# Hybrid streaming encoder step: fewer pieces made early at a mixer's end, an earlier reciprocal, and sums of squares on one engine

## The chip, the cores and the metric

The kernel runs on one core of one Trainium2 chip. A core has a matmul engine (PE), three engines for elementwise work (DVE, ACT, POOL), and queues for transfers; SP's queue carries nearly all weight loads here. Each engine works through its own instructions strictly in program order and waits on semaphores for the others. The metric is device time in microseconds; the kernel before takes 1227.7 us (median of 3 runs, 1226.74 to 1227.85).

## The reference

One inference step of a two-layer trunk over 304 tokens (16 meta, 256 prompt, 32 sample), width 1024, in fp32. Cut to what matters here:

```python
def half_ffn(x, g_pre, w_in, w_out, g_post):
    gate, up = jnp.split(rmsnorm(x, g_pre) @ w_in, 2, axis=-1)
    return x + 0.5 * rmsnorm((jax.nn.silu(gate) * up) @ w_out, g_post)

for l in range(DEPTH):                                   # DEPTH = 2
    x = half_ffn(x, norm_ffn1_pre[l], ffn1_w_in[l], ffn1_w_out[l], norm_ffn1_post[l])
    z = rmsnorm(x, norm_mix_pre[l]) @ w_in[l]            # attention q k v, retention q k v, gate
    mix = concat(windowed_attention(z), groupnorm(retention(z)) * silu(gate))
    x = x + rmsnorm(mix @ w_out[l], norm_mix_post[l])
    x = half_ffn(x, norm_ffn2_pre[l], ffn2_w_in[l], ffn2_w_out[l], norm_ffn2_post[l])
y = rmsnorm(x, final_norm)                               # plus caches and retention states
```

Every sub-layer ends with an RMS norm of its output, so its sum of squares over all 1024 features must be known before the residual can be formed, and the next sub-layer starts with another norm.

## The kernel before

**Pieces.** Activations lie transposed, features on the 128 partitions and tokens along the free axis. A weight comes from memory in chunks of 128x1024 fp32 (tile `raw`, 4 buffers, so a load can only start when both halves of the chunk four places ahead of it have been read). Each half of a chunk is a piece of 128x512. A piece is made by two instructions: ACT writes a rounded copy `hi` (line 206) and DVE the rest `lo = raw - hi` (line 209). PE multiplies every piece in three passes, weights hi with activations hi (line 258), lo with hi (259), hi with lo (261). Pieces go into a ring of 10 buffers and at most 8 may lie made and unused. For the places where one sub-layer ends and the next begins, extra buffers are opened (`xhi`, `xlo`), so that the first `EXTRA` pieces of the next sub-layer can be made early on top of the ring's 8; that number is line 68, and `edges` lists the four places.

**Order of the work.** The Python program writes instructions in its own order, and each engine keeps that order. `tick` advances a model clock after each step of matmuls, lets `advance` make the next pieces, and runs what has fallen due in the list `later`. So where pieces are made decides what stands in front of the norm's instructions in ACT's and DVE's queues.

**End of a mixer** (function `mixer`). The two gate products (`done_g`) are followed by `gate_out`: for each of four blocks ACT applies silu, DVE multiplies (line 1147), ACT copies to hi (1148), DVE forms lo (1149). Then come two groups of matmuls with `w_out`, each over eight blocks of the input (the four attention blocks first, the four gated ones last) and four output blocks. `Post.done0` handles the first group's outputs as they finish: ACT squares (512), DVE scales by the norm's gain (513), POOL adds the squares into `acc` (515). `Post.done1` does so for the second group, with the additions on DVE (525, 527). `finish` sums over the partitions with four matmuls of ones (533, 534), split around PE's matmuls for the retention state (line 826: 8 ahead, 56 behind). After that `pre_norm` of the next sub-layer follows: POOL scales x by s (547), DVE and ACT form the new activations (562, 565, 425, 428).

**The factor s.** x is kept multiplied by the norm's s for a while, and `unscale` divides it out again: a reciprocal on DVE (line 571, tile `rs`), and eight products on POOL (line 574, one per block of x). In a mixer, `unscale` stands after `gate_out`; in the feed-forwards it runs out of the list `later`, or in the last one before the third group of matmuls.

Of the kernel before, what the change touches and what calls it, by code (L numbers as in the profile page):

```python
# [12 lines left out]
ALU = mybir.AluOpType  # L13
# [51 lines left out]
R_NORM = 2663  # L65
R_KT = 7100
UNSCALE = 1500
EXTRA = 8
RAWS = 4


# [36 lines left out]
def tile_hybrid_step(ctx, tc, I, O):  # L108
    nc = tc.nc
    PE, ACT, DVE, POOL, SP = nc.tensor, nc.scalar, nc.vector, nc.gpsimd, nc.sync  # L110
# [11 lines left out]
    chunks = []  # L122
# [22 lines left out]
    edges = []  # L145
    for l in range(DEPTH):
        if l:
            edges.append(2 * len(chunks))
        ch_ffn_in(I["ffn1_w_in"][l])
        ch_cols(I["ffn1_w_out"][l], 512, KF)  # L150
        ch_cols(I["ffn1_w_out"][l], 0, KF)
        edges.append(2 * len(chunks))
        ch_qkv(I["w_in"][l])
        for c0 in (C_Q + 256, C_RK, C_RQ, C_RV, C_RK + 256, C_RQ + 256, C_RV + 256, C_G, C_G + 256):
            ch_pair(I["w_in"][l], c0)
        ch_cols(I["w_out"][l], 512, KD)
        ch_cols(I["w_out"][l], 0, KD)
        edges.append(2 * len(chunks))
        ch_ffn_in(I["ffn2_w_in"][l])
        ch_cols(I["ffn2_w_out"][l], 512, KF)  # L160
        ch_cols(I["ffn2_w_out"][l], 0, KF)


    extra = {b + j for b in edges for j in range(EXTRA)}
    ring = [0]
    for i in range(2 * len(chunks)):
        ring.append(ring[-1] + (i not in extra))
# [62 lines left out]
    clock = [0.0]  # L230
    later = []
# [205 lines left out]
    def small(name, tag=None, bufs=1):  # L437
        return ap.tile([P, N], F32, tag=tag or name, bufs=bufs, name=name)
# [59 lines left out]
    T0 = 0  # L498


    class Post:
        def __init__(self, post, nxt):
            self.post, self.nxt = post, nxt
            self.yg = acts(4, F32)
            self.acc = small("acc")
            self.b2 = None
            self.last = None

        def done0(self, m, bk):
            y = bk[m][:, :N - T0]  # L510
            sq = ap.tile([P, N], F32, tag="sq", bufs=2, name="sq") if m else self.acc
            ACT.activation(out=sq[:, T0:], in_=y, func=ACTF.Square)  # L512
            DVE.tensor_scalar(out=self.yg[m][:, T0:], in0=y, scalar1=gain(*self.post, 4 + m), scalar2=None, op0=ALU.mult)
            if m:
                POOL.tensor_tensor(out=self.acc[:, T0:], in0=self.acc[:, T0:], in1=sq[:, T0:], op=ALU.add)  # L515

        def done1(self, m, bk):
            self.bk = bk
# [41 lines left out]
        def step(self, k):  # L560
# [5 lines left out]
            if k == KD - 1:  # L566
                ACT.activation(out=self.se[:, T0:], in_=self.s[:, T0:], func=ACTF.Square, scale=EPS ** 0.5)

        def unscale(self):
            rs = small("rs")  # L570
            DVE.reciprocal(out=rs[:, T0:], in_=self.s[:, T0:])  # L571

            def part(k):
                POOL.tensor_tensor(out=x[:, k, T0:], in0=x[:, k, T0:], in1=rs[:, T0:], op=ALU.mult)  # L574
            for k in range(KD):
                later.append((clock[0] + UNSCALE * k, lambda k=k: part(k)))
            later.sort(key=lambda e: e[0])


    def ffn(pre, post, nxt, prev, after=None):  # L580
# [5 lines left out]
        with tc.tile_pool(name="ffn", bufs=1, reuse_waits="tile") as fp, ExitStack() as late:  # L586
# [22 lines left out]
            for g in range(KF // 2):  # L609
                if g == 1:  # L610
# [6 lines left out]
                    for j in range(2):  # L617
                        pair(0, j, bk)
                if g == 2 and prev and last:
                    prev.unscale()  # L620
                if g == 2 and not prev:
                    late_loads()
# [3 lines left out]
                    fin.x_in(*divmod(g - 4, 2))  # L626
                bk = group4(KD, xh, xl, n, (0, 2, 1, 3), done(g), lead=2 if prev and g == 0 else 1)
            if prev and not last:
                later.append((clock[0] + UNSCALE, prev.unscale))
            if not last:  # L630
                open_extra()
            p = Post(post, nxt)
# [101 lines left out]
    def mixer(l, prev):  # L734
# [431 lines left out]
        if lastl:  # L1166
            T0 = NMETA
        n = N - T0
        group2(xh, xl, n, done_g(0))
        group2(xh, xl, n, done_g(1))  # L1170
        flush()
# [1 line left out]
        mtmp.close()  # L1173
        open_extra()
        prev.unscale()
        p = Post((3, l), (4, l))
        ox, lx = (lambda k: mh[k][:, T0:]), (lambda k: ml[k][:, T0:])
        group4(KD, ox, lx, n, range(4), p.done0)
        ACT.preload_act_table(ACTF.Sqrt)
# [12 lines left out]
    prev = None  # L1192
# [32 lines left out]
```

## Time and profile before

| | |
|---|---|
| median of 3 runs | 1227.7 us |
| profiled execution: time, span | 1228.38 us, 1226.6 us |
| PE busy | 1179.8 us, 96% of the span |
| DVE busy | 825.1 us, 67% |
| ACT busy | 593.7 us, 48% |
| POOL busy | 193.0 us, 16% |
| TensorE clock granted, mean | 0.986 of full |
| DMA | 182.51 MB, 149 GB/s over the span |

PE is busy nearly all the time, so time is lost or won where PE stands still or runs at its lower clock. The span is 1.8 us shorter than the execution's own time, and that time 0.7 us above the median.

### The profile page before, as it was taken

Reading aid. Unit: us, or ns where it says so; the run is one execution under the profiler, and the core shown is the slowest. Engines: PE = TensorE matmul, PEld = TensorE weight load, DVE = VectorE, ACT = ScalarE, POOL = GpSimd, SP = SyncE. Lnnn points to the kernel's source line nnn. Section 1 sums busy time; section 2 is a strip of 40 time slices with the busy share of each in tenths; the row PEclk is TensorE's granted clock in tenths of the full one; section 3 lists DMA queues with packets and bytes.
Section 4 is the critical chain, followed back from the end, with each engine's and each line's share of the span. In section 5 each row is a group of like instructions: output and inputs, shape, how many; then the busy total and the mean of one; then the engine's idle time right before and its main releaser. Section 6 shows DMA issues by size and latency. Waiting matters only on the chain. (4 is left out here: it accounts for less than half of the span.)

```text
span 1226.6 us, 22759 instructions
## 1 busy us (share of the span) xinstructions
PE 1179.8 (96%) x8716; PEld 1148.3 (94%) x8716; DVE 825.1 (67%) x1491; ACT 593.7 (48%) x1211; POOL 193.0 (16%) x205
## 2 busy tenths in 40 slices
PE   8999999999997999999999999999999879999995
PEld 8999999998896999999989999998989869999995
DVE  6766654677777766665576665757767877766543
ACT  6544544555446544444454444455544554554442
POOL 4200001220234300013030000313111443000000
PEclk9999999999998999999999999999999989999997
DMA  7655465723425364545716455556344435645531
GB/s 223 173 178 164 138 189 157 240 74 114 124 87 172 87 189 138 159 157 165 224 36 189 138 158 182 161 162 201 108 108 117 123 118 151 205 140 173 188 104 39
DMA packets 155309, 182.51 MB, mean 149 GB/s; under 512 B 12016, under 2 KB 125984, under 8 KB 154944
## 3 DMA queue, kind: packets, MB, share of 16 engines
q1 hardware_dynamic: 153488, 178.84, 47.8%
q0 software_dynamic: 1344, 1.76, 0.8%
q8 instruction: 68, 1.11, 0.4%
q10 hardware_dynamic: 368, 0.47, 0.1%
q14 instruction: 41, 0.34, 0.1%
HBM read 175.70 MB, written 2.23 MB: 145 GB/s over the span
## 5 line engine op out<-in xcount | busy, mean ns | idle before, releaser
L209 DVE TENSOR_TENSOR lo<-raw,hi 128x512 fp32r<-128x512 f32 x608 | 419.1, 733 | 131.8 <-ACT hi L206 128.0
L258 PE MATMUL bk<-act,hi 128*128 128x304 f32 (+1 forms) x1664 | 504.8, 305 | 0.3 <-ACT act L425 0.3
L259 PE MATMUL bk<-act,lo 128*128 128x304 f32 (+1 forms) x1664 | 496.0, 300 | 0.8 <-DVE lo L209 0.8
L261 PE MATMUL bk<-act,hi 128*128 128x304 f32 (+1 forms) x1664 | 479.1, 300 | 1.3 <-DVE act L428 1.3
L206 ACT ACTIVATE hi<-raw 128x512 fp32r<-128x512 f32 x607 | 348.1, 622 | 143.4 <-PE bk L261 104.7
L258 PEld LDWEIGHTS bk<-act,hi 128*128 128x128 f32 x1664 | 312.9, 188 | 5.9 <-issue 3.5
L259 PEld LDWEIGHTS bk<-act,lo 128*128 128x128 f32 x1664 | 313.0, 188 | 2.0 <-DVE lo L209 1.5
L261 PEld LDWEIGHTS bk<-act,hi 128*128 128x128 f32 x1664 | 306.7, 188 | 2.0 <-DVE act L428 2.0
L258 PE MATMUL bk<-hh,hi 128*128 128x304 f32 (+1 forms) x704 | 210.7, 300 | 0.0
L259 PE MATMUL bk<-hh,lo 128*128 128x304 f32 (+1 forms) x704 | 210.2, 299 | 0.0
L261 PE MATMUL bk<-hl,hi 128*128 128x304 f32 (+1 forms) x704 | 207.8, 301 | 0.0
L595 ACT ACTIVATE sg<-tg 128x304 f32<-128x304 f32 (+1 forms) x88 | 40.0, 455 | 199.6 <-DVE tg L594 199.6
L258 PEld LDWEIGHTS bk<-hh,hi 128*128 128x128 f32 x704 | 132.5, 188 | 0.0
L259 PEld LDWEIGHTS bk<-hh,lo 128*128 128x128 f32 x704 | 132.3, 188 | 0.0
L261 PEld LDWEIGHTS bk<-hl,hi 128*128 128x128 f32 x704 | 131.0, 188 | 0.0
L594 DVE TENSOR_TENSOR tg<-bk,rb 128x304 f32<-128x304 f32 (+1 forms) x88 | 41.0, 466 | 86.3 <-PE bk L261 86.1
L574 POOL TENSOR_TENSOR x<-x,rs 128x304 f32<-128x304 f32 (+1 forms) x40 | 46.6, 1197 | 309.6 <-DVE rs L571 309.6
L599 DVE TENSOR_TENSOR hl<-tu,hh 128x304 fp32r<-128x304 f32 (+1 forms) x88 | 41.5, 471 | 50.9 <-ACT hh L598 45.0
L598 ACT ACTIVATE hh<-tu 128x304 fp32r<-128x304 f32 (+1 forms) x88 | 40.0, 455 | 59.5 <-DVE tu L597 59.5
L515 POOL TENSOR_TENSOR acc<-acc,sq 128x304 f32<-128x304 f32 (+1 forms) x18 | 15.7, 870 | 322.6 <-ACT sq L512 321.8
L547 POOL TENSOR_TENSOR x<-x,s 128x304 f32<-128x304 f32 (+1 forms) x35 | 31.3, 930 | 140.9 <-PE bk L295 109.3
L258 PE MATMUL bk<-act,xhi 128*128 128x304 f32 (+1 forms) x160 | 49.6, 315 | 2.8 <-ACT act L425 2.6
(239 smaller groups left out, 1116.5 us busy)
## 6 DMA issues: line engine op xcount, KB each, us to landing
raw<-in_ffn_w_in_dram SPq DMA_DIRECT2D x352, 256.0 KB, 4.7
raw<-in_ffn_w_out_dram SPq DMA_DIRECT2D x88, 512.0 KB, 4.9
raw<-in_w_in_dram SPq DMA_DIRECT2D x36, 512.0 KB, 4.1
raw<-in_w_out_dram SPq DMA_DIRECT2D x16, 512.0 KB, 3.8
raw<-in_w_in_dram SPq DMA_DIRECT2D x16, 256.0 KB, 3.1
dec<-in_dec_dram SPq DMA_DIRECT2D x2, 1280.0 KB, 8.3
t<-t SPq DMA_DIRECT2D x24, 76.0 KB, 2.1
out_dram<-xgm SPq DMA_DIRECT2D x2, 384.0 KB, 3.6
```

The source lines that it names most:

```text
L206: ACT.activation(out=hi, in_=r, func=ACTF.Copy)
L209: DVE.tensor_tensor(out=lo, in0=r, in1=hi.bitcast(F32), op=ALU.subtract)
L258: PE.matmul(out=out, lhsT=a, rhs=xh, start=first, stop=False)
L259: PE.matmul(out=out, lhsT=b, rhs=xh, start=False, stop=False)
L261: PE.matmul(out=out, lhsT=a, rhs=xl, start=False, stop=last)
L515: POOL.tensor_tensor(out=self.acc[:, T0:], in0=self.acc[:, T0:], in1=sq[:, T0:], op=ALU.add)
L547: POOL.tensor_tensor(out=x[:, j, T0:], in0=x[:, j, T0:], in1=self.s[:, T0:], op=ALU.mult)
L574: POOL.tensor_tensor(out=x[:, k, T0:], in0=x[:, k, T0:], in1=rs[:, T0:], op=ALU.mult)
L594: DVE.tensor_tensor(out=tg[:, T0:], in0=bk[j][:, :n], in1=rb[:, T0:], op=ALU.mult)
L595: ACT.activation(out=sg[:, T0:], in_=tg[:, T0:], func=ACTF.Silu)
L598: ACT.activation(out=hh[a][:, T0:], in_=tu[:, T0:], func=ACTF.Copy)
L599: DVE.tensor_tensor(out=hl[a][:, T0:], in0=tu[:, T0:], in1=hh[a][:, T0:].bitcast(F32), op=ALU.subtract)
```

## The change

Three edits. The edge at a mixer's end gets 4 extra pieces, the other edges keep 8. `unscale` is cut in two: `inverse` makes the reciprocal, and in a mixer it is now written in front of the gate's matmuls, with the eight products where they were; in the feed-forwards that use `later`, the reciprocal stays at its time and the products come one step of 1500 model ns behind it. And `Post` takes the engine for the additions in `done0`; a mixer passes DVE.

```diff
--- before.py
+++ after.py
@@ -65,7 +65,7 @@
 R_NORM = 2663
 R_KT = 7100
 UNSCALE = 1500
-EXTRA = 8
+EXTRA = (8, 4)
 RAWS = 4
 
 
@@ -145,23 +145,23 @@
     edges = []
     for l in range(DEPTH):
         if l:
-            edges.append(2 * len(chunks))
+            edges.append((2 * len(chunks), EXTRA[0]))
         ch_ffn_in(I["ffn1_w_in"][l])
         ch_cols(I["ffn1_w_out"][l], 512, KF)
         ch_cols(I["ffn1_w_out"][l], 0, KF)
-        edges.append(2 * len(chunks))
+        edges.append((2 * len(chunks), EXTRA[0]))
         ch_qkv(I["w_in"][l])
         for c0 in (C_Q + 256, C_RK, C_RQ, C_RV, C_RK + 256, C_RQ + 256, C_RV + 256, C_G, C_G + 256):
             ch_pair(I["w_in"][l], c0)
         ch_cols(I["w_out"][l], 512, KD)
         ch_cols(I["w_out"][l], 0, KD)
-        edges.append(2 * len(chunks))
+        edges.append((2 * len(chunks), EXTRA[1]))
         ch_ffn_in(I["ffn2_w_in"][l])
         ch_cols(I["ffn2_w_out"][l], 512, KF)
         ch_cols(I["ffn2_w_out"][l], 0, KF)
 
 
-    extra = {b + j for b in edges for j in range(EXTRA)}
+    extra = {b + j for b, e in edges for j in range(e)}
     ring = [0]
     for i in range(2 * len(chunks)):
         ring.append(ring[-1] + (i not in extra))
@@ -499,8 +499,8 @@
 
 
     class Post:
-        def __init__(self, post, nxt):
-            self.post, self.nxt = post, nxt
+        def __init__(self, post, nxt, eng=POOL):
+            self.post, self.nxt, self.eng = post, nxt, eng
             self.yg = acts(4, F32)
             self.acc = small("acc")
             self.b2 = None
@@ -512,7 +512,7 @@
             ACT.activation(out=sq[:, T0:], in_=y, func=ACTF.Square)
             DVE.tensor_scalar(out=self.yg[m][:, T0:], in0=y, scalar1=gain(*self.post, 4 + m), scalar2=None, op0=ALU.mult)
             if m:
-                POOL.tensor_tensor(out=self.acc[:, T0:], in0=self.acc[:, T0:], in1=sq[:, T0:], op=ALU.add)
+                self.eng.tensor_tensor(out=self.acc[:, T0:], in0=self.acc[:, T0:], in1=sq[:, T0:], op=ALU.add)
 
         def done1(self, m, bk):
             self.bk = bk
@@ -566,12 +566,13 @@
             if k == KD - 1:
                 ACT.activation(out=self.se[:, T0:], in_=self.s[:, T0:], func=ACTF.Square, scale=EPS ** 0.5)
 
+        def inverse(self):
+            self.rs = small("rs")
+            DVE.reciprocal(out=self.rs[:, T0:], in_=self.s[:, T0:])
+
         def unscale(self):
-            rs = small("rs")
-            DVE.reciprocal(out=rs[:, T0:], in_=self.s[:, T0:])
-
             def part(k):
-                POOL.tensor_tensor(out=x[:, k, T0:], in0=x[:, k, T0:], in1=rs[:, T0:], op=ALU.mult)
+                POOL.tensor_tensor(out=x[:, k, T0:], in0=x[:, k, T0:], in1=self.rs[:, T0:], op=ALU.mult)
             for k in range(KD):
                 later.append((clock[0] + UNSCALE * k, lambda k=k: part(k)))
             later.sort(key=lambda e: e[0])
@@ -617,6 +618,7 @@
                     for j in range(2):
                         pair(0, j, bk)
                 if g == 2 and prev and last:
+                    prev.inverse()
                     prev.unscale()
                 if g == 2 and not prev:
                     late_loads()
@@ -626,7 +628,8 @@
                     fin.x_in(*divmod(g - 4, 2))
                 bk = group4(KD, xh, xl, n, (0, 2, 1, 3), done(g), lead=2 if prev and g == 0 else 1)
             if prev and not last:
-                later.append((clock[0] + UNSCALE, prev.unscale))
+                later.append((clock[0] + UNSCALE, prev.inverse))
+                later.append((clock[0] + 2 * UNSCALE, prev.unscale))
             if not last:
                 open_extra()
             p = Post(post, nxt)
@@ -1166,6 +1169,7 @@
         if lastl:
             T0 = NMETA
         n = N - T0
+        prev.inverse()
         group2(xh, xl, n, done_g(0))
         group2(xh, xl, n, done_g(1))
         flush()
@@ -1173,7 +1177,7 @@
         mtmp.close()
         open_extra()
         prev.unscale()
-        p = Post((3, l), (4, l))
+        p = Post((3, l), (4, l), DVE)
         ox, lx = (lambda k: mh[k][:, T0:]), (lambda k: ml[k][:, T0:])
         group4(KD, ox, lx, n, range(4), p.done0)
         ACT.preload_act_table(ACTF.Sqrt)
```

The first place is DVE at the end of the first mixer, from the gate's last instruction to the last pieces of `w_out`; `osb` is the retention output, `act` an activation buffer. Before:

```order
L1149 TENSOR_TENSOR act<-osb,act 128x304
L571 RECIPROCAL rs<-s 128x304
L209 TENSOR_TENSOR lo<-raw,hi 128x512 x6
L513 TENSOR_SCALAR act<-bk,gcol 128x304 x4
L209 TENSOR_TENSOR lo<-raw,hi 128x512 x2
```

And now, with line numbers moved by the new lines:

```order
L1152 TENSOR_TENSOR act<-osb,act 128x304
L209 TENSOR_TENSOR lo<-raw,hi 128x512 x6
L513 TENSOR_SCALAR act<-bk,gcol 128x304 x2
L515 TENSOR_TENSOR acc<-acc,sq 128x304
L513 TENSOR_SCALAR act<-bk,gcol 128x304
L515 TENSOR_TENSOR acc<-acc,sq 128x304
L513 TENSOR_SCALAR act<-bk,gcol 128x304
L515 TENSOR_TENSOR acc<-acc,sq 128x304
L209 TENSOR_TENSOR lo<-raw,hi 128x512 x2
```

The reciprocal has left this place (it stands in front of the last retention blocks now), and three additions have come from POOL.

The second place is ACT in the second group of `w_out`, from the extra pieces to the norm's square root (line 538). Before:

```order
L206 ACTIVATE xhi_4599<-raw 128x512
L206 ACTIVATE xhi_4603<-raw 128x512
L206 ACTIVATE hi<-raw 128x512 x4
L525 ACTIVATE sq<-bk 128x304
L206 ACTIVATE hi<-raw 128x512 x2
L525 ACTIVATE sq<-bk 128x304 x3
L206 ACTIVATE hi<-raw 128x512 x2
L538 ACTIVATE bk<-bk,epst 128x304
```

And now:

```order
L206 ACTIVATE xhi_4553<-raw 128x512
L206 ACTIVATE xhi_4557<-raw 128x512
L206 ACTIVATE hi<-raw 128x512 x6
L525 ACTIVATE sq<-bk 128x304 x4
L206 ACTIVATE hi<-raw 128x512 x2
L538 ACTIVATE bk<-bk,epst 128x304
```

In front of the last of the four squares stood 8 extra and 6 ring pieces; now it is 4 and 6. The four pieces that are left over come after the statistics of the next sub-layer, in front of its first gate products.

The third place is POOL, from its last product of the group norm (`gsd` is that norm's factor) to the next sub-layer. Before:

```order
L925 TENSOR_TENSOR osb<-osb,gsd 128x304 x3
L574 TENSOR_TENSOR x<-x,rs 128x304 x7
L515 TENSOR_TENSOR acc<-acc,sq 128x304
L574 TENSOR_TENSOR x<-x,rs 128x304
L515 TENSOR_TENSOR acc<-acc,sq 128x304 x2
L521 TENSOR_SCALAR xg<-x,gcol 128x304
```

And now:

```order
L800 TENSOR_TENSOR qr<-t_3961,t_3963 128x608
L928 TENSOR_TENSOR osb<-osb,gsd 128x304 x3
L575 TENSOR_TENSOR x<-x,rs 128x304 x8
L521 TENSOR_SCALAR xg<-x,gcol 128x304
L547 TENSOR_TENSOR x<-x,s 128x304 x7
```

The eight products of x follow straight on the group norm, with no additions among them.

## Rows read from the trace of the kernel before

**Rows 1.** Who waited for whom: total us, times, longest us.

```profile
PE bk L533 <- DVE acc L527: 19.0, 5, 9.5
```

**Rows 2.** Timeline of PE, first mixer's end: start, us, instruction, [idle before, releaser].

```profile
358.94 0.30 PE L261 MATMUL bk<-act,hi 128*128 128x304 f32 x1
...
372.55 0.41 PE L259 MATMUL bk<-act,lo 128*128 128x304 f32 x1 [0.24 <-DVE lo L209]
...
375.30 0.30 PE L261 MATMUL bk<-act,hi 128*128 128x304 f32 x1
375.54 0.68 PE L826 MATMUL bk<-vt,k 128*64 128x64 f32 x8
384.86 1.38 PE L533 MATMUL bk<-acc,ones 128*128 128x304 f32 x2 [8.64 <-DVE acc L527]
...
406.10 0.30 PE L258 MATMUL bk<-act,hi 128*128 128x304 f32 x1
```

**Rows 3.** Timeline of PE, second mixer's end.

```profile
975.08 0.40 PE L259 MATMUL bk<-act,lo 128*128 128x288 f32 x1 [0.53 <-DVE lo L209]
...
988.12 1.33 PE L533 MATMUL bk<-acc,ones 128*128 128x288 f32 x2 [9.53 <-DVE acc L527]
```

**Rows 4.** Timeline of PE, end of the first feed-forward.

```profile
234.79 0.30 PE L261 MATMUL bk<-hl,hi 128*128 128x304 f32 x1
235.38 0.78 PE L533 MATMUL bk<-acc,ones 128*128 128x304 f32 x2 [0.28 <-DVE acc L527]
...
255.50 0.30 PE L258 MATMUL bk<-act,hi 128*128 128x304 f32 x1
```

**Rows 5.** Timeline of ACT, first mixer's end.

```profile
369.11 0.42 ACT L512 ACTIVATE sq<-bk 128x304 f32<-128x304 f32 x1 [7.54 <-POOL acc L515]
...
371.89 3.24 ACT L206 ACTIVATE xhi<-raw 128x512 fp32r<-128x512 f32 x6
...
378.47 0.63 ACT L206 ACTIVATE hi<-raw 128x512 fp32r<-128x512 f32 x1 [1.51 <-DMA raw<-in_ffn_w_in_dram]
...
381.43 0.41 ACT L525 ACTIVATE sq<-bk 128x304 f32<-128x304 f32 x1
```

**Rows 6.** Timeline of DVE, from the last retention blocks to the next feed-forward.

```profile
334.43 0.69 DVE L209 TENSOR_TENSOR lo<-raw,hi 128x512 fp32r<-128x512 f32 x1 [2.29 <-ACT hi L206]
...
352.34 0.46 DVE L1147 TENSOR_TENSOR osb<-osb,zg 128x304 f32<-128x304 f32 x1
...
357.54 0.47 DVE L1149 TENSOR_TENSOR act<-osb,act 128x304 fp32r<-128x304 f32 x1 [0.53 <-ACT act L1148]
357.93 2.04 DVE L571 RECIPROCAL rs<-s 128x304 f32<-128x304 f32 x1
359.90 6.87 DVE L209 TENSOR_TENSOR lo<-raw,hi 128x512 fp32r<-128x512 f32 x6
366.69 1.41 DVE L513 TENSOR_SCALAR act<-bk,gcol 128x304 f32<-128x304 f32 x3
...
413.10 0.48 DVE L599 TENSOR_TENSOR hl<-tu,hh 128x304 fp32r<-128x304 f32 x1 [3.08 <-POOL qr L843]
...
416.00 3.70 DVE L209 TENSOR_TENSOR lo<-raw,hi 128x512 fp32r<-128x512 f32 x6
```

**Rows 7.** Timeline of POOL, first mixer's end.

```profile
349.70 0.84 POOL L925 TENSOR_TENSOR osb<-osb,gsd 128x304 f32<-128x304 f32 x1 [4.00 <-DVE gsd L924]
360.06 8.22 POOL L574 TENSOR_TENSOR x<-x,rs 128x304 f32<-128x304 f32 x7 [9.52 <-DVE rs L571]
```

**Rows 8.** Timeline of DVE, a sum and a product with both inputs in SBUF.

```profile
394.43 1.11 DVE L565 TENSOR_TENSOR x<-x,act 128x304 f32<-128x304 f32 x1
...
1037.17 0.81 DVE L597 TENSOR_TENSOR tu<-tu,sg 128x288 f32<-128x288 f32 x1 [0.21 <-ACT sg L595]
```

**Rows 9.** Stretches: us, busy (count) of PE, PEld, DVE, ACT, POOL, PEclk, DMA share, GB/s.

```profile
376.00:385.00 9.00, 0.36 (x5) 0.22 (x3) 6.91 (x12) 6.19 (x13) 0.00 (x0) 0.73 0.98 304
385.00:391.00 6.00, 6.00 (x61) 4.78 (x62) 3.51 (x7) 2.24 (x5) 2.10 (x3) 0.55 0.78 240
```

## The prediction

> **What bounds the kernel now.** PE is busy 96% of the span, so I looked for the places where it is not. The list of waits comes first: of all waits on PE the longest by far is that of the norm's sum (L533) for the additions of squares on DVE (L527), 19.0 us over five times, none above 9.5 [rows 1]. The timeline of PE says which ones matter: 8.64 us at the first mixer's end, 9.53 at the second's [rows 2, 3], against 0.28 at a feed-forward's end [rows 4], where the same instructions stand. So two places hold nearly all of PE's idle time, and the reader is to see that in each PE has finished its matmuls (last of them at 375.30) and has only eight small ones left to do until 384.86.
>
> What is late there is read on ACT. The square of block 0 comes at 381.43, though its bank was complete some 2.5 us ahead of 375.30. In front of it in ACT's queue are a square that waited 7.54 us for POOL's additions, until 369.11, then two pieces, eight extra pieces and four more, the latter also waiting for their loads [rows 5]; two more stand between the squares. DVE shows why all began late: the gate ends at 357.54, then come a reciprocal of 2.04 us and six pieces that take 6.87 us, while six pieces elsewhere take 3.70 [rows 6]. Beside the 6.87 POOL runs its products of x, seven in 8.22 us [rows 7]. DVE and POOL hinder each other there.
>
> The wait has a second price. In the 9 us of it the granted clock is 0.73, in the 6 us behind it 0.55, near the lower of the two levels (1.2 against 2.4 GHz) [rows 9]. From L533 to the ninth piece of the next sub-layer takes 406.10 - 384.86 = 21.24 us here, 255.50 - 235.38 = 20.12 where PE had hardly stood still [rows 2, 4].
>
> **The change part by part.** All times are of the first mixer; both ends have the same shape.
>
> *What PE would need if nothing were late.* Last matmul at 375.30, less its own stall of 0.24 on a piece [rows 2], is 375.06. To L533 a feed-forward takes 235.38 - 234.79 = 0.59 [rows 4], and the eight state matmuls 0.68 [rows 2]: 376.33. That is 8.5 us before 384.86, the most that this end can give by itself.
>
> *Reciprocal moved.* It leaves the place behind the gate, where 2.04 us stood on the path. It now stands in front of the retention blocks, some 6 us before the idle 2.29 us of DVE at 334.43 [rows 6], which takes it up; PE needs the results pushed by it only several us later. Cost 0, and 2.0 each if that cover is gone.
>
> *Products of x moved.* They no longer wait for the reciprocal, so POOL starts them when its last group-norm product ends, 349.70 + 0.84 = 350.54 instead of 360.06 [rows 7]. The six pieces behind the gate are freed (6.87 to 3.70). But the products now run beside the gate. Eight of them at 0.84 (alone) to 1.17 (8.22/7) take 6.7 to 9.4 us; at 1.1, until 359.4. The gate's eight DVE instructions, 352.34 to 358.01, take two SBUF inputs each. No row has them beside a busy POOL. The nearest rows: the gate's own take 0.46 alone [rows 6], others of their kind 1.11 or 0.81 beside POOL [rows 8], so 0.35 to 0.65 more for each; 0 is the bound below (an overlap can't make them faster). I take 0.5, between the two rows, for the six that fall before 359.4: the gate ends at 361.0. PE wants its last result at 358.94 [rows 2], so the margin is 0.93 and PE stalls 3.0 - 0.9 = 2.1 us, and so do the matmuls behind it. Bounds: 0, and 8 x 0.65 - 0.9 = 4.3.
>
> The Trainium skill, page "SBUF — State Buffer", section "Who interferes with whom", has a rule that speaks against this edit: a DVE instruction with two SBUF inputs and a GpSimd instruction that reads SBUF exclude one another for a whole instruction, and whichever started first goes first. The trace agrees as far as it goes: DVE's scalings of PSUM (one SBUF input at most) run at 1.41/3 = 0.47 beside POOL [rows 6], while the pieces nearly double. By the rule a gate instruction could wait a whole product of 0.84, eight of them 6.7 us, and the stall would be 5.8 instead of at most 4.3, some 1.5 us per mixer more.
>
> *Additions on DVE.* POOL's additions are gone, and with them ACT's wait until 369.11. DVE gets three more at about 0.47. Now the last square of the first group waits for DVE: six pieces from 361.0 (3.7), two scalings and an addition (1.4), 366.1, still 3.0 earlier.
>
> *Four early pieces fewer.* From that square ACT then has 12.3 us of work and waits to 381.43 before, and 4 pieces fewer now in front of the first squares, with two more moved ahead of them; by 0.4 for the square, 1.1 for two pieces, 1.3 for the table load behind them, and ten pieces at 3.24/6 = 0.54, it can be at the squares at 374.3 plus what it waits for loads. Loads can start some 2 us earlier, as raw buffers are freed earlier, and five chunks instead of seven must arrive before the last square. Waits on loads in front of the squares were about 2 us (one of 1.51 [rows 5]); I keep 2: 376.3. PE's last matmul starts at 375.06 + 2.1 = 377.2, so ACT is just in time for the last block. DVE, with pieces and additions one behind another, adds some 0.5 at the end. L533 starts at 376.33 + 2.1 + 0.5 = 378.9, 5.9 us earlier.
>
> *Where the four pieces go.* They stand between the reciprocal of the next norm and the first gate product of the feed-forward, about 4 x 0.62 = 2.5 us on DVE. Behind them the third of the products there waited 3.08 us for POOL's state until 413.10 [rows 6]; that wait shrinks by what they take, so the pieces of 416.00 stay where they were. From 358.94 to 375.30 PE starts 114 matmuls, 16.12 us without the stall, 0.141 each [rows 2]. It needs the first of the four when its ninth to twelfth pieces are through, 4 x 12 matmuls behind 406.10, at 412.9; they are made by about 411. Cost 0; 2.5 per mixer if the wait on POOL gave nothing, and still behind PE's margin.
>
> *Clock.* PE no longer stands 8.6 us, so the stretch behind L533 should come to the 20.12 of the feed-forward: 1.1 us.
>
> *Feed-forwards.* The products come one step later in a group of 22 pieces, 264 matmuls at 0.141, 37 us, in which POOL is otherwise idle: 0.
>
> *Sum.* First mixer 5.9 + 1.1 = 7.0. The second waited 0.9 longer (9.53 against 8.64) and stalled 0.53 on a piece instead of 0.24, which goes too: 7.0 + 0.9 + 0.3 = 8.2. Together 15.2 us. The profiled execution took 1228.4 (span 1226.6), 0.7 above the median of 1227.7; from the median I forecast 1212.5.
>
> **The rivals.** *Gate undisturbed:* POOL and DVE miss one another, as the gate's instructions start 1.4 us apart with gaps. Then the 2.1 and the 0.5 fall away: 8.5 + 1.1 = 9.6 and 10.8, 20.4 us, 1207.3. Against it: POOL's products have no gaps, and every two-input instruction beside such a row was slower [rows 8]. *Gate at its worst:* 4.3 instead of 2.1 on each, 10.8 us in all, 1217; by the page's rule 1.5 more each, 1220.
>
> *Loads decide:* at 376 to 385 the DMA engines are 98% busy at 304 GB/s [rows 9]. If the squares still wait for their chunks, only the four pieces (2 chunks of 0.52 MB, 3.4 us at 304 GB/s) are saved, with 1.1 for the clock, so 4.5 each, 9 us, 1218.7. Against it: until the pieces behind the gate are read no load can start for want of buffers, and that moves forward.
>
> *The edit of the pieces does nothing but move them:* PE then waits for the first pieces of the feed-forward instead. Four pieces late by their whole time on DVE, 2.5 us, and the wait on POOL not hiding them: 15.2 - 5 = 10, 1217.5. The margin of 1.9 us at 412.9 speaks against it.
>
> *Slower:* the stall in the gate lets the clock fall. The second group of `w_out` is 96 matmuls at 0.141 us, 13.5 us, and twice that at half the clock. If it stayed low through all of it, L533 would come at 378.9 + 13.5 = 392.4, 7.5 later than before; without the 1.1, 7.5 and 6.3 us, 1241.5. It decides from about 6 us of low clock in that group. Against it: stalls of 0.24 and 0.53 left the clock alone, and 2.1 is nearer to these than to 8.64. The Trainium skill, "TensorE: Matmul & The Clock Gate", section "Loop structure matters more than you think", warns of waits between bursts of matmuls; which of the two a 2 us stall is, no row here shows.
>
> **How the numbers follow.** Forecast (1209 to 1216 around 1212.5): 0.55. Gate undisturbed: 0.17. Gate at its worst, loads, or late pieces, 1216 to 1221: 0.20. No change or little of it, by two of these at once: 0.04. Slower: 0.04. The range from 1205.5 to 1219.5 leaves out the last two and the tail of the third. 0.2% is 2.5 us, about what a measurement of this kernel tells from no change: faster 0.92, the same 0.04, slower 0.04.
>
> **What would show it.** Right: PE's idle time before L533 at 1 to 3 us at both mixer ends; granted clock near 1 behind it; the six pieces behind the gate at about 3.7 us; POOL's products starting at the last group-norm product; the gate's DVE instructions at 0.8 to 1.1 us and PE stalling about 2 us in the last blocks of the first `w_out` group. Wrong: L533 still waiting 5 us or more; a stall of PE in the first two groups of a second feed-forward; a granted clock of about one half in the second `w_out` group.

## The result, and the profile after

The changed kernel takes 1210.58 us (median of 4 runs, 1210.19 to 1211.73) against 1227.23 for the kernel before (4 runs, 1226.74 to 1227.85): a ratio of 0.9866, 95% interval 0.9849 to 0.9883. The forecast was 1212.5, the range 1205.5 to 1219.5. The profiled execution took 1210.19 us, its span is 1208.4 instead of 1226.6, the mean granted clock 0.995 instead of 0.986. Line numbers behind line 569 are up to 3 higher than before.

The list of waits on PE (total us, times, longest) shows the norm's sum, 19.0 us in [rows 1], at 2.3, and one new entry: the first matmul that uses a gated block waits for ACT's rounded copy of it.

```profile
PE bk L533 <- DVE acc L527: 2.3, 4, 1.4
PE bk L258 <- ACT act L1151: 1.7, 2, 0.9
```

The timeline of PE at the first mixer's end (start, us, instruction, idle before it and what ended it) has the new stall in the first `w_out` group, and no idle time at all ahead of L533, where 8.64 us stood [rows 2]. The row of 396.52 is the next sub-layer's ninth piece.

```profile
358.95 0.41 PE L258 MATMUL bk<-act,hi 128*128 128x304 f32 x1 [0.87 <-ACT act L1151]
...
375.42 0.30 PE L261 MATMUL bk<-act,hi 128*128 128x304 f32 x1
...
376.31 0.78 PE L533 MATMUL bk<-acc,ones 128*128 128x304 f32 x2
...
396.52 0.30 PE L258 MATMUL bk<-act,hi 128*128 128x304 f32 x1
...
952.83 0.40 PE L258 MATMUL bk<-act,hi 128*128 128x288 f32 x1 [0.80 <-ACT act L1151]
...
970.84 0.75 PE L533 MATMUL bk<-acc,ones 128*128 128x288 f32 x2 [1.40 <-DVE acc L527]
```

From 952.83 it is the second mixer: the same stall, and 1.40 us in front of L533 instead of 9.53 [rows 3].

ACT's timeline says why. The fourth square of the first group waits 1.59 us instead of 7.54 [rows 5]; from there to the second group's squares it has two pieces, a table load and ten more pieces, and loses 0.73 us to a load; and the last two squares wait for PE's matmuls. At the second mixer (967.21) the last two pieces wait 1.53 us for their load, and the third square then waits for DVE: from this come the 1.40.

```profile
364.54 0.42 ACT L512 ACTIVATE sq<-bk 128x304 f32<-128x304 f32 x1 [1.59 <-DVE acc L515]
...
372.60 1.39 ACT L206 ACTIVATE hi<-raw 128x512 fp32r<-128x512 f32 x2 [0.73 <-DMA raw<-in_ffn_w_in_dram]
373.89 0.72 ACT L525 ACTIVATE sq<-bk 128x304 f32<-128x304 f32 x2
375.19 0.42 ACT L525 ACTIVATE sq<-bk 128x304 f32<-128x304 f32 x1 [0.58 <-PE bk L259]
375.77 0.42 ACT L525 ACTIVATE sq<-bk 128x304 f32<-128x304 f32 x1 [0.16 <-PE bk L261]
...
967.21 1.37 ACT L206 ACTIVATE hi<-raw 128x512 fp32r<-128x512 f32 x2 [1.53 <-DMA raw<-in_ffn_w_in_dram]
...
969.76 0.41 ACT L525 ACTIVATE sq<-bk 128x288 f32<-128x288 f32 x1 [0.59 <-DVE acc L527]
```

DVE's timeline has the reciprocal in its new place (327.86) with idle time still left behind it (0.83 us at 333.70; 2.29 before, [rows 6]). In the gate the products (L1150) of blocks 2 to 4 take 1.11 us instead of 0.46, while the subtractions (L1152) keep about 0.5. The six pieces behind the gate take 3.70, not 6.87. In the next feed-forward the 3.08 us wait for POOL [rows 6] is gone: L600 there waits 0.58 us, for ACT.

```profile
327.86 2.05 DVE L571 RECIPROCAL rs<-s 128x304 f32<-128x304 f32 x1
...
351.60 0.59 DVE L1150 TENSOR_TENSOR osb<-osb,zg 128x304 f32<-128x304 f32 x1
...
353.15 1.11 DVE L1150 TENSOR_TENSOR osb<-osb,zg 128x304 f32<-128x304 f32 x1
354.78 0.52 DVE L1152 TENSOR_TENSOR act<-osb,act 128x304 fp32r<-128x304 f32 x1 [0.52 <-ACT act L1151]
355.23 1.11 DVE L1150 TENSOR_TENSOR osb<-osb,zg 128x304 f32<-128x304 f32 x1
...
358.93 0.47 DVE L1152 TENSOR_TENSOR act<-osb,act 128x304 fp32r<-128x304 f32 x1 [0.52 <-ACT act L1151]
359.45 3.70 DVE L209 TENSOR_TENSOR lo<-raw,hi 128x512 fp32r<-128x512 f32 x6
...
404.14 0.48 DVE L600 TENSOR_TENSOR hl<-tu,hh 128x304 fp32r<-128x304 f32 x1 [0.58 <-ACT hh L599]
...
407.05 3.70 DVE L209 TENSOR_TENSOR lo<-raw,hi 128x512 fp32r<-128x512 f32 x6
```

POOL's timeline, asked for in narrow stretches so that each product of x has a row of its own, has them straight behind the group norm. Those beside the gate take 1.07, where one of this size alone takes 0.84 [rows 7].

```profile
352.86 1.07 POOL L575 TENSOR_TENSOR x<-x,rs 128x304 f32<-128x304 f32 x1
353.89 1.08 POOL L575 TENSOR_TENSOR x<-x,rs 128x304 f32<-128x304 f32 x1
354.93 1.07 POOL L575 TENSOR_TENSOR x<-x,rs 128x304 f32<-128x304 f32 x1
```

The stretches of [rows 9] (us, busy and count of PE, PEld, DVE, ACT, POOL, granted clock, DMA share, GB/s) have PE at work and the clock at its upper level, 2.4 GHz, in all three; the first row is the second `w_out` group, behind the stall in the gate.

```profile
369.00:376.00 7.00, 7.00 (x55) 6.82 (x54) 6.35 (x12) 5.36 (x11) 0.00 (x0) 1.00 0.86 265
376.00:385.00 9.00, 8.50 (x93) 6.85 (x91) 7.18 (x13) 4.11 (x10) 5.69 (x7) 1.00 0.62 201
385.00:391.00 6.00, 5.87 (x40) 5.62 (x41) 5.96 (x9) 3.31 (x8) 4.89 (x6) 1.00 0.00 0
```

### The profile page after: what moved, and what is told of

Same layout as the page of the kernel before. It is cut to its first block, busy times and chain, and to the rows that moved or that the text cites. A ratio compares the mean times of both kernels' runs of the same rounds, so it can differ in the third digit from the quotient of the medians.

```text
span 1208.4 us, 22774 instructions
## 1 busy us (share of the span) xinstructions
PE 1177.9 (97%) x8716; PEld 1146.5 (95%) x8716; DVE 823.1 (68%) x1497; ACT 593.0 (49%) x1211; POOL 185.4 (15%) x199
## 3 DMA queue, kind: packets, MB, share of 16 engines
q8 instruction: 68, 1.11, 0.4%
## 5 line engine op out<-in xcount | busy, mean ns | idle before, releaser
L258 PE MATMUL bk<-act,hi 128*128 128x304 f32 (+1 forms) x1696 | 515.0, 305 | 2.0 <-ACT act L1151 1.7
L259 PE MATMUL bk<-act,lo 128*128 128x304 f32 (+1 forms) x1696 | 505.3, 300 | 0.0
L261 PE MATMUL bk<-act,hi 128*128 128x304 f32 (+1 forms) x1696 | 489.0, 300 | 2.2 <-DVE act L428 2.2
L206 ACT ACTIVATE hi<-raw 128x512 fp32r<-128x512 f32 x615 | 352.0, 622 | 140.8 <-PE bk L261 103.0
L258 PEld LDWEIGHTS bk<-act,hi 128*128 128x128 f32 x1696 | 318.9, 188 | 8.2 <-issue 3.5
L259 PEld LDWEIGHTS bk<-act,lo 128*128 128x128 f32 x1696 | 319.0, 188 | 0.9 <-DVE lo L209 0.2
L261 PEld LDWEIGHTS bk<-act,hi 128*128 128x128 f32 x1696 | 312.7, 188 | 3.7 <-DVE act L428 3.2
L600 DVE TENSOR_TENSOR hl<-tu,hh 128x304 fp32r<-128x304 f32 (+1 forms) x88 | 41.5, 471 | 46.2 <-ACT hh L599 46.2
L515 POOL TENSOR_TENSOR acc<-acc,sq 128x304 f32<-128x304 f32 (+1 forms) x12 | 10.1, 838 | 321.0 <-ACT sq L512 320.4
L598 DVE TENSOR_TENSOR tu<-tu,sg 128x304 f32<-128x304 f32 (+1 forms) x88 | 43.5, 494 | 14.5 <-ACT sg L596 9.4
```

Source lines behind the costliest of these rows:

```text
L206: ACT.activation(out=hi, in_=r, func=ACTF.Copy)
L258: PE.matmul(out=out, lhsT=a, rhs=xh, start=first, stop=False)
L259: PE.matmul(out=out, lhsT=b, rhs=xh, start=False, stop=False)
L261: PE.matmul(out=out, lhsT=a, rhs=xl, start=False, stop=last)
L598: DVE.tensor_tensor(out=tu[:, T0:], in0=tu[:, T0:], in1=sg[:, T0:], op=ALU.mult)
L600: DVE.tensor_tensor(out=hl[a][:, T0:], in0=tu[:, T0:], in1=hh[a][:, T0:].bitcast(F32), op=ALU.subtract)
```

## The experiments

Twelve kernels ran, each beside the kernel before, whose medians lay between 1227.23 and 1227.74. Medians, and ratios to the before of the same measurement with their 95% intervals:

| kernel | early reciprocal | additions | early pieces at a mixer's end | us | ratio |
|---|---|---|---|---|---|
| before | no | POOL | 8 | 1227.2 | 1 |
| additions alone | no | DVE | 8 | 1226.94 | 0.9994 (0.9985 to 1.0003) |
| pieces alone | no | POOL | 4 | 1221.79 | 0.9954 (0.9941 to 0.9966) |
| reciprocal undone | no | DVE | 4 | 1220.14 | 0.994 (0.9927 to 0.9952) |
| reciprocal alone | yes | POOL | 8 | 1216.9 | 0.9916 (0.9902 to 0.9929) |
| pieces undone | yes | DVE | 8 | 1220.05 | 0.994 (0.9926 to 0.9953) |
| six pieces | yes | DVE | 6 | 1215.6 | 0.9903 (0.9888 to 0.9918) |
| changed kernel | yes | DVE | 4 | 1210.58 | 0.9866 (0.9849 to 0.9883) |
| additions undone | yes | POOL | 4 | 1210.2 | 0.986 (0.9846 to 0.9873) |
| two pieces | yes | DVE | 2 | 1210.49 | 0.9862 (0.9849 to 0.9876) |
| products early too | yes | DVE | 4 | 1207.47 | 0.9837 (0.9824 to 0.9851) |
| the same, additions on POOL | yes | POOL | 4 | 1207.38 | 0.9837 (0.9823 to 0.985) |
| the same, two pieces | yes | DVE | 2 | 1207.91 | 0.9842 (0.9829 to 0.9856) |

The twelfth, 58 more matmuls in the kernel before, stands at the end of this section. All that are made from the changed kernel keep its later products in the feed-forwards; pieces alone and additions alone do not have them.

### One part undone at a time

**Pieces undone** in the changed kernel:

```diff
-EXTRA = (8, 4)
+EXTRA = (8, 8)
```

> The changed kernel with 8 extra pieces at a mixer's end again, the other two edits kept. My theory: ACT reaches its last square of the first w_out group at the same time as in the changed kernel (364.5), then has 14 pieces instead of 10 in front of the last square of the second group. It needed 15.2 us for that stretch before, so the last square comes near 380, L533 some 4 us later at each mixer's end, and some of the clock's 1.1 us is lost: 1219, 8 to 9 us above the changed kernel. Rival, that the early reciprocal alone freed the queue and the number of pieces does not matter: within 2 us of 1210.6.

Measured 1220.05, 9.5 us more. In its first mixer pieces wait 0.71, 1.33 and 0.57 us for loads (0.73 in the changed kernel), the squares begin 3.3 us later than in the changed kernel, and L533 waits again. PE's timeline, and ACT's:

```profile
380.66 0.99 PE L533 MATMUL bk<-acc,ones 128*128 128x304 f32 x2 [4.09 <-DVE acc L527]
```

```profile
375.50 0.63 ACT L206 ACTIVATE hi<-raw 128x512 fp32r<-128x512 f32 x1 [1.33 <-DMA raw<-in_ffn_w_in_dram]
```

**Reciprocal undone:** it stands behind the gate again, in front of the products.

```diff
-        prev.inverse()
         group2(xh, xl, n, done_g(0))
...
         open_extra()
+        prev.inverse()
         prev.unscale()
```

> The changed kernel with the reciprocal back behind the gate, pieces and additions as changed. My theory: the gate is undisturbed (its DVE products at 0.46 us, no stall of PE there), but the reciprocal's 2.04 us and the six pieces beside POOL (6.9 instead of 3.7 us) return, ACT's last square of the first group comes near 368, the squares of the second group near 377.5, L533 3 to 4 us later than in the changed kernel at each mixer's end: 1217 to 1218. Rival, that the reciprocal's place only trades one loss for another (the stall in the gate against the slower pieces): within 1.5 us of 1210.6.

Measured 1220.14, 9.6 us more, some 2 above what was expected. The gate is quick again and PE doesn't stall in it. Behind it everything is as late as before: the six pieces take 6.89 us on DVE, and ACT's fourth square comes at 369.17, against 369.11 in [rows 5], only that it now waits for DVE and not for POOL. DVE, then ACT:

```profile
360.33 6.89 DVE L209 TENSOR_TENSOR lo<-raw,hi 128x512 fp32r<-128x512 f32 x6
```

```profile
369.17 0.42 ACT L512 ACTIVATE sq<-bk 128x304 f32<-128x304 f32 x1 [7.17 <-DVE acc L515]
```

So moving the additions does not end ACT's wait; it only changes the name of the engine waited for.

**Additions undone:** POOL adds the first group's squares again.

```diff
-        p = Post((3, l), (4, l), DVE)
+        p = Post((3, l), (4, l))
```

> The changed kernel with the three additions back on POOL, pieces and reciprocal as changed. My theory: POOL is done with its products of x by 358, before the first square exists, so ACT's fourth square no longer waits for it, and the additions' engine is worth nothing: 1210.6 within 1 us, ACT's wait on POOL for that square under 2 us where it was 7.5. Rival, that the additions on DVE are what took ACT's wait of 7.5 us away: 4 us or more slower at each mixer's end, 1218.

Measured 1210.2, the same as the changed kernel. ACT's fourth square waits 0.93 us, for POOL. The stall in the gate falls from 0.87 to 0.21 us, but L533 now waits 0.49 and 1.23 us, and the time stays.

### One part alone

**Pieces alone**, in the kernel before; the list `edges` carries the number as in the change.

```diff
-EXTRA = 8
+EXTRA = (8, 4)
```

> The kernel before with 4 extra pieces at a mixer's end and nothing else changed. My theory: ACT is still held until 369.1 by POOL's additions, which stand behind the late products of x, and then has 10 pieces instead of 14, 9.4 us instead of 15.2 to the last squares: L533 near 379.5, 5 us earlier at each mixer's end, with about half of the clock's gain: 1216 to 1217. Rival, that the edits only work together (each queue is held by something else as long as one is missing): 2 us or less faster than before, 1225 or more.

Measured 1221.79, some 5 us above what was expected: 5.4 us gained, little more than half of what undoing the pieces costs. ACT's fourth square still waits 7.56 us for POOL. With four pieces fewer behind it, the loads are what it meets next, 0.65 and 1.33 us (at 375.39 and 378.05), and L533 still waits 5.92. ACT's timeline:

```profile
368.72 0.43 ACT L512 ACTIVATE sq<-bk 128x304 f32<-128x304 f32 x1 [7.56 <-POOL acc L515]
```

**Reciprocal alone:** the changed kernel with the two other edits undone.

```diff
-EXTRA = (8, 4)
+EXTRA = (8, 8)
...
-        p = Post((3, l), (4, l), DVE)
+        p = Post((3, l), (4, l))
```

> Only the reciprocal's move: eight early pieces at every edge, additions of the first group back on POOL. Theory (the engine of the additions is worth nothing once the products of x start early; the two other edits carry all of it): as with only the pieces undone, 1220.0 +- 1. Rival (the additions on DVE are worth about 1.6 us, the difference between the run with a late reciprocal and DVE's additions, 1220.1, and the run with four pieces alone, 1221.8): 1221.7.

Measured 1216.9, which neither theory expected: 10.3 us gained, and 3.1 less time than the same kernel with the additions on DVE (1220.05). The trace shows two reasons, which no run tests apart. POOL's queue now holds seven products, then an addition that waits for ACT's squares, then, at 364.04, the eighth product:

```profile
350.64 7.28 POOL L575 TENSOR_TENSOR x<-x,rs 128x304 f32<-128x304 f32 x7
362.95 1.15 POOL L515 TENSOR_TENSOR acc<-acc,sq 128x304 f32<-128x304 f32 x1 [5.03 <-ACT sq L512]
```

So no product runs beside the last gate block, whose DVE product takes 0.46 again, and PE's stall there is 0.21 instead of 0.86. And DVE is spared three additions, so that ACT's fourth square waits 0.94 us and not 1.59. At each mixer that makes some 0.6 us in the gate and 0.7 to 1.0 in the wait of L533 (3.42 and 4.39 us against 4.09 and 5.40), 2.9 in all. Of these the spans keep 1.7 (1216.5 against 1218.2). This execution reached the first gate 0.65 us later (352.48 against 351.83), though the two kernels do the same up to there; the rest may be the clock, granted at 0.64 from 376 to 385 us here and at 0.81 in the other, which is not shown. It was the longest of its runs (1218.27), so the trace shows just over half of the 3.1 between the medians.

**Additions alone**, in the kernel before; `Post` takes the engine as in the change.

```diff
-        p = Post((3, l), (4, l))
+        p = Post((3, l), (4, l), DVE)
```

> Only the additions of the mixer's first group on DVE, in the kernel before; the reciprocal stays behind the gate, eight early pieces. Theory (DVE is late itself, behind the reciprocal and six pieces of 6.87 us, so ACT's fourth square waits as long for DVE, until 369.17 in the run with only the reciprocal undone, as for POOL, 369.11): no change, 1227 +- 1. Rival A (the difference between four pieces alone, 1221.8, and four pieces with these additions, 1220.1): 1225.6. Rival B (the additions cost 3 us wherever eight pieces follow, as between 1216.9 and 1220.05 with the early reciprocal): 1230.

Measured 1226.94: no change, as the theory had it. ACT's timeline:

```profile
368.28 0.43 ACT L512 ACTIVATE sq<-bk 128x304 f32<-128x304 f32 x1 [7.16 <-DVE acc L515]
```

By the table the early reciprocal alone (-10.3) and the pieces alone (-5.4) add up to 15.7, and both together without the third edit gain 17.0. The third edit is worth nothing alone, nothing beside the other two, about -1.7 beside the pieces alone (1221.79 to 1220.14), and +3.1 beside the reciprocal alone.

### How many pieces

**Six and two** in the changed kernel; the second has 2 in the same place.

```diff
-EXTRA = (8, 4)
+EXTRA = (8, 6)
```

> The changed kernel with 6 extra pieces at a mixer's end instead of 4. My theory: PE's matmuls and ACT's queue ended within half a microsecond of one another with 4, so each further piece shows fully: two pieces at 0.55 to 0.7 us of ACT and some wait on loads, 1.5 to 2.5 us at each end: 1214 to 1215.5, on the way to the 1220 with 8. Rival, that the loss at 8 comes from the squares being split by two ring pieces, which 6 does not do: 1211 or less.

> The changed kernel with 2 extra pieces at a mixer's end instead of 4. My theory: at the first mixer's end PE itself is last, so nothing is won; at the second, PE's wait of 1.40 us for squares behind a late load goes in most part: 1209.5. Rival, that the two pieces now missing are wanted by PE in the second group of the feed-forward before DVE has made them: a new stall there and 1212 or more.

Measured 1215.6 (the profiled run is the longest of the four, 1217.92) and 1210.49. The waits on PE, six first, then two:

```profile
PE bk L533 <- DVE acc L527: 7.8, 5, 3.6
```

```profile
PE bk L533 <- DVE acc L527: 0.9, 3, 0.3
PE bk L259 <- DVE lo L209: 0.6, 2, 0.3
```

From eight to six and from six to four each pair saves 4.5 and 5.0 us, 2.2 to 2.5 per mixer, half of that for each piece. From four to two the wait of L533 falls by another 1.4, but PE waits 0.6 for pieces in the feed-forwards behind the mixers. The stretches behind the two L533 are 1.1 and 0.8 us longer than in the changed kernel's trace, and the time does not change.

### The gate

**Products early too:** `unscale` directly behind `inverse`, in front of the gate's matmuls.

```diff
         prev.inverse()
+        prev.unscale()
         group2(xh, xl, n, done_g(0))
...
         open_extra()
-        prev.unscale()
```

> The changed kernel with the eight products of x also written in front of the gate's matmuls, so that POOL does six of them some 20 us ahead of the gate and two between its last two group-norm products. My theory: the gate's DVE products fall from 1.1 to 0.46 us, PE's stalls of 0.87 and 0.80 us in the first w_out group vanish, and ACT and DVE come 2 us earlier to the second mixer's squares, which takes part of PE's wait of 1.40 us there: 1208.5, 2 us faster than the changed kernel. Rival, that the products only move their collision to the pieces and scores of the retention blocks and to POOL's group-norm products: within 0.5 us of 1210.6 or slower, with a new stall of PE ahead of the gate.

Measured 1207.47, 3.1 us less than the changed kernel. The products now stand between POOL's group-norm products, where POOL waited before (the last two are shown; a group-norm product follows at 349.61), and the gate has DVE to itself: its blocks follow at 1.41 us (353.62, 355.03), not at 2.08 (353.15, 355.23). POOL, DVE, and PE's longest wait for the norm:

```profile
345.57 2.07 POOL L575 TENSOR_TENSOR x<-x,rs 128x304 f32<-128x304 f32 x2
```

```profile
352.24 0.46 DVE L1150 TENSOR_TENSOR osb<-osb,zg 128x304 f32<-128x304 f32 x1
...
353.62 0.47 DVE L1150 TENSOR_TENSOR osb<-osb,zg 128x304 f32<-128x304 f32 x1
...
355.03 0.48 DVE L1150 TENSOR_TENSOR osb<-osb,zg 128x304 f32<-128x304 f32 x1
```

```profile
PE bk L533 <- DVE acc L527: 1.8, 4, 0.9
```

Both stalls in the gate are gone, and 0.45 of the wait of L533 at the second mixer (0.95 instead of 1.40). The stalls had cost PE 1.35 and 1.29 us, as is worked out below, so this makes 3.1. The spans differ by 2.5, as this execution reached the first gate 0.64 later (352.24 against 351.60).

**On top of it, in two kernels, POOL's additions and two pieces:**

```diff
-        p = Post((3, l), (4, l), DVE)
+        p = Post((3, l), (4, l))
```

```diff
-EXTRA = (8, 4)
+EXTRA = (8, 2)
```

> Products of x right behind the early reciprocal (as in the run at 1207.5) and the additions of the first group on POOL instead of DVE. With the products out of the way POOL is free behind the gate. Theory: 1207.5 +- 0.7, the engine of the additions is worth nothing. Rival: POOL's three additions of 0.84 slow the pieces beside them (two took 2.39 instead of 1.29 when the additions were on POOL) and ACT waits up to 0.9 longer: 1208.5 to 1209.5.

> Products of x right behind the early reciprocal, and two early pieces at a mixer's end instead of four. The wait left in front of the norm's sum at the second mixer's end (0.95 with four) should go. Theory (what is saved there is paid back in the next feed-forward, whose pieces then come later, as with two pieces in the changed kernel, 1210.5 against 1210.6): 1207.4. Rival (the 0.9 counts in full): 1206.5.

Measured 1207.38 and 1207.91: neither gives anything more. With two pieces L533 waits 0.9 us in all, and pieces are waited for elsewhere again (0.6). The version at 1207.4 beats both kernels.

### The clock by itself

**58 matmuls more at each mixer's end**, in the kernel before; they write to the norm's bank ahead of the sum, which overwrites them.

```diff
-        def finish(self):
+        def finish(self, busy=None):
             b = bank()
+            for _ in range(58 if busy else 0):
+                PE.matmul(out=b[:, T0:N], lhsT=busy[:, T0:T0 + P], rhs=busy[:, T0:], start=True, stop=True)
...
-        p.finish()
+        p.finish(mh[7])
```

> The kernel before with 58 matmuls put in front of the norm's sum at each mixer's end, whose results are overwritten: they fill PE's idle 8.6 and 9.5 us without touching any other engine. My theory: the granted clock stays near 1 through the sum and the state matmuls behind it, and the stretch from L533 to the ninth piece of the next feed-forward falls from 21.2 to about 20.1 us: 2.2 us faster than the kernel before in all, 1225.0. Rival, that the clock is worth nothing because the activations behind it are paced by DVE: the same as before within 0.5 us. Other rival, that the clock is most of the gain: 10 us faster or more.

Measured 1227.16, ratio 0.9998 (0.9989 to 1.0006): no difference in the median. The runs spread more than in any other kernel, 1225.73 to 1229.77, with 4 of 11 at 1225.7 to 1225.9. The profiled one is of these, 1225.84, and has the clock at 1.00 in both stretches of [rows 9]:

```profile
376.00:385.00 9.00, 8.33 (x61) 8.02 (x59) 6.88 (x12) 5.98 (x13) 0.00 (x0) 1.00 0.97 308
385.00:391.00 6.00, 5.94 (x75) 5.08 (x76) 4.45 (x8) 2.41 (x5) 3.04 (x4) 1.00 0.77 235
```

PE's timeline has the norm's sum (L535 here) and the next sub-layer's ninth piece:

```profile
385.03 0.78 PE L535 MATMUL bk<-acc,ones 128*128 128x304 f32 x2 [0.70 <-DVE acc L527]
...
405.17 0.30 PE L258 MATMUL bk<-act,hi 128*128 128x304 f32 x1
```

The stretch between them is 20.14 us instead of 21.24, and at the second mixer 19.25 (986.08 to 1005.33) instead of 20.32 (988.12 [rows 3] to 1008.44), with the other engines' work unchanged. So in this execution the low clock's price is 1.1 us per mixer. The median shows none of it: the other seven runs lie at 1226.9 to 1229.8, with a mean granted clock of 0.992 to 0.995 against 0.995 to 0.996 in the four, and what lengthened them is not known, as they left no trace.

## Why the prediction was right

The forecast was 15.2 us less, by the spans it came to 18.2. Split at the same points:

| from the traces, before minus after | forecast | measured |
|---|---|---|
| ahead of the first mixer's gate: 352.34 [rows 6] - 351.60 | 0 | 0.74 |
| from there to L533: (384.86 [rows 2] - 376.31) - 0.74 | 5.9 | 7.8 |
| L533 to the ninth piece: 21.24 - (396.52 - 376.31) | 1.1 | 1.0 |
| from there to the second L533: (988.12 [rows 3] - 970.84) - (406.10 [rows 2] - 396.52) | 7.1 | 7.7 |
| from there to the end of the span: 18.2 - 17.28 | 1.1 | 0.9 |

Of the 3.0 us above the forecast 2.5 lie in the stretches up to the two L533 and 0.7 ahead of the first gate. No edit earned these 0.7: at the end of the first feed-forward, where nothing was changed, the trace is already 0.72 ahead (234.07 against 234.79 [rows 4]), and the runs of the kernel before lie 1.1 apart themselves. The medians fell by 16.7 us, 1.5 more than forecast, as the profiled execution of before stood 1.1 above its new median and that of after 0.4 below.

At the first mixer the 1.9 us above the forecast are three terms: 0.62 in what PE would need, 0.75 in the gate, and 0.5 for a tail that did not come. These are PE's rows, of the kernel before and then of the changed one:

```profile
354.91 0.30 PE L258 MATMUL bk<-act,hi 128*128 128x304 f32 x1
...
361.46 0.30 PE L261 MATMUL bk<-act,hi 128*128 128x304 f32 x1
...
372.01 0.30 PE L258 MATMUL bk<-act,hi 128*128 128x304 f32 x1
...
372.80 0.31 PE L261 MATMUL bk<-act,hi 128*128 128x304 f32 x1
```

```profile
354.17 0.30 PE L258 MATMUL bk<-act,hi 128*128 128x304 f32 x1
...
359.46 0.41 PE L261 MATMUL bk<-act,hi 128*128 128x304 f32 x1
...
362.07 0.30 PE L261 MATMUL bk<-act,hi 128*128 128x304 f32 x1
```

*What PE would need: 0.62 too much.* The stall on a piece cost 0.51, not the 0.24 of its wait: PE takes 0.79 from 372.01 to 372.80, for two steps of 0.14. And the 0.59 taken from a feed-forward holds a wait of 0.28 [rows 4]; here the state matmuls start 0.24 behind the last matmul [rows 2]. So the need was 375.30 - 0.51 + 0.24 + 0.68 = 375.71 instead of 376.33. Less the 0.74 and with the 1.35 of the next paragraph this gives 376.32; L533 came at 376.31.

*Gate stall: the mechanism was right, the size was not.* 2.1 us were forecast. PE's wait is 0.87 and 0.80, but here too it lost more than its wait: from the first matmul on a gated block to the last of that group it takes 362.07 - 354.17 = 7.90 us instead of 361.46 - 354.91 = 6.55, and at the second mixer 7.53 instead of 6.24, so 1.35 and 1.29. Of six instructions slowed by 0.5 only the products of four blocks were slowed, by 0.13 and three times 0.65; with the subtractions the gate lost 2.13 us (the last subtraction starts at 358.93, and 357.54 [rows 6] less 0.74 is 356.80) instead of 3.0. The margin of 0.93 held: 2.13 - 0.93 = 1.20, and the matmul that needs DVE's last result (358.94 [rows 2], 358.20 without the 0.74) starts at 359.46, 1.26 later. The estimate of 5.8 by the rule of the Trainium skill ("SBUF — State Buffer", "Who interferes with whom") is far off; why is told at the end.

*Additions on DVE: wrongly credited.* The prediction said that with POOL's additions gone ACT's wait until 369.11 was gone with them. What removed it is the early reciprocal: with the additions alone on DVE the square comes at 368.28, with the reciprocal undone at 369.17; with the reciprocal early and POOL adding, ACT waits 0.94. The sum held because both edits were in it.

*Pieces, loads and the tail.* ACT was expected at the squares at 374.3 plus 2 us of loads; 373.89 plus the drift of 0.74 is 374.6, with 0.73 for loads at the first mixer, and the tail of 0.5 did not appear there. At the second they took 1.7 (1.53 in the row at 967.21) and the tail was 1.40. That the loads follow the freeing of the raw buffers is borne out: from 350 to 384 us the queue of SP, which starts them, waited for DVE's subtractions most of all, in the kernel before:

```profile
SPq L188 <- DVE lo L209: 17.2, 4, 10.2
```

With four pieces and the late reciprocal ACT waited 2.0 and 1.2 us for loads (pieces alone, reciprocal undone), with the early one 0.7. The four pieces that moved cost nothing, as said: the wait on POOL of 3.08 is gone and the six pieces of 416.00 [rows 6] start at 407.05, 8.95 earlier, where L533 is 8.55 earlier.

*Clock.* 1.0 and 0.9 behind the two L533, forecast 1.1 each. That this is the clock is shown by one execution, the profiled one with 58 more matmuls, where the same stretch shrinks by 1.1 at both mixers; its median shows no gain.

*Feed-forwards.* No run takes their later products alone. From the ninth piece to the second mixer's first gate product the traces take 955.54 - 406.10 = 549.44 and 945.89 - 396.52 = 549.37 us: 0, as forecast.

*The rivals.* Gate undisturbed fell with the rows at 1.11, though the kernel without the disturbance came out at 1207.4, what that rival forecast. Loads decide and pieces only moved would have left waits of several us at L533 or in the feed-forward; neither is there. For the slower rival the granted clock would have had to fall behind the stall: from 369 to 376 us it is 1.00.

## What to carry to other kernels

When a queue is late, name the first thing in it that is late, not the last releaser: moving the additions that ACT waited for to another engine changed, by itself, the name in the brackets and no time, while taking a 2 us reciprocal out of the path moved everything behind it. What runs beside an instruction belongs to its price: the products of x were free in POOL's idle time between the group-norm products, and cost 3 us one step later. Cut a reserve of work made early until the wait in front of the norm ends, and no further: eight to four saved 9.5 us, four to two nothing.

## What the runs showed of the hardware

**DVE and POOL fall into step.** Beside back-to-back products of x the gate's blocks follow each other at 2.08 us, just two products (352.86 to 354.93 is 2.07). DVE's product starts at 353.15 while one of POOL's (352.86) runs, and ends at 354.26: 0.65 of wait and the usual 0.46. POOL's next one, of 353.89, takes 1.08 instead of 0.85. The subtraction, 0.52 us later, finds POOL almost through and loses 0.05. The Trainium skill, "SBUF — State Buffer", section "Who interferes with whom", states that the one that comes second waits for the other's whole instruction; these rows agree to 0.13 us (353.93, where POOL's product ends, plus 0.46 is 354.39), and show why eight instructions cost 2.13 us and not 6.7: DVE's pauses for ACT fall on POOL's products. One product of POOL less beside the gate was worth 0.65 in PE's wait, 0.86 with pieces undone and 0.21 with the reciprocal alone.

**The clock and waits of different lengths.** Behind the stall of 1.40 us the granted clock stayed at 1.00 (the matmuls of L533 took 0.75 for two). After a wait of 3.30, in the profiled run with six pieces, the stretch from 376 to 382 has 0.74, and the two matmuls took 1.38:

```profile
376.00:382.00 6.00, 2.70 (x11) 1.41 (x9) 4.01 (x7) 3.34 (x8) 0.00 (x0) 0.74 0.95 311
```

After 8.64 us it was 0.55 for 6 us more [rows 9]. The length of the wait alone does not order the rows: behind 4.09 us, with pieces undone, the two matmuls took 0.99 and the stretch from 376 to 385 has 0.81, while behind 3.42, with the reciprocal alone, they took 1.38 and it has 0.64.
